# The second product of an MLP on four PSUM banks, one for each token tile, in place of three, and the first product on four in place of five

## The chip, the cores and the metric

The kernel runs on one core of a Trainium2 chip. The core has five engines that run side by side, each through its own list of instructions in order: TensorE (PE) for matrix products, VectorE (DVE) and GpSimd (POOL) for sums of tiles, ScalarE (ACT) for copies and nonlinear functions, and SyncE (SP), which here only issues transfers. An instruction waits for those of other engines through semaphores. Products of PE land in PSUM, which the kernel divides into eight banks of 128 x 512 fp32 values; the other tiles lie in SBUF, the on-chip memory.

The metric is the device time of one execution in microseconds (us); lower is better. Times are given as the median of several runs. One further execution is taken with a hardware profiler, and all rows below come from that one.

## What is computed

The model is a decoder layer: attention and a state space model side by side, then an MLP. The change lies in the MLP. Cut to that part, the reference is

```python
h = rmsnorm(x, pre_mlp_g[i]) * (1.0 + sc2) + sh2
f = jnp.square(jax.nn.relu(h @ w_mlp_in[i])) @ w_mlp_out[i]
x = x + g2 * rmsnorm(f, post_mlp_g[i])
```

with x of 1024 tokens x 1024 features, `w_mlp_in` 1024 x 4096 and `w_mlp_out` 4096 x 1024, all fp32.

## The kernel before

**Precision.** Each fp32 operand is split into a rounded part hi and the rest lo. `parts` (line 1081) does this: ACT copies the source to hi (line 1082), DVE subtracts to get lo (line 91, the helper `tt` that issues every sum). `mm3` (line 83) makes a product out of three matmuls, hi x hi, hi x lo and lo x hi (lines 86, 87, 88), which follow each other on PE. One call of `mm3` is called a product of three matmuls below.

**Pairs.** The 4096 hidden features are cut into 32 chunks of 128, and two chunks make a pair. Within a pair both matrix products of the MLP are done as a Strassen-Winograd scheme of 2 x 2 blocks: seven block products in place of eight, at the price of sums of blocks before and after. `pair_in(p)` (line 1171) makes the hidden features of pair p out of the first weight; its PSUM tiles are called `fi`, its weight blocks `w` (a ring of six), its raw weight tiles `w1r`. It gives the results to `f`: ACT copies, DVE adds, ACT takes relu and square. `BANK` (line 1168) says which of four accumulators a, b, c and f each block product goes to. a is in use from the first block product (P1) to the last but one (P4), whose result ACT reads at line 1215.

`pair_out(p)` (line 1330) multiplies the hidden features of pair p with the second weight. Its block products are numbered i = 0 to 6, and each has four token tiles t = 0 to 3: 28 steps (i,t) a pair, in the order of the list `STEPS`. Step (i,t) takes its operands from `ops[(7 p + i) % 3]` (two of these three buffers show as `ops` in the profile, the third as `h2s`), puts its product into the PSUM tile `q[t]`, shown as `fo`, and calls `collect`, which adds it to the running sum n of that token tile (`facc`):

```python
if first:
    q[t] = psR("BBD", "fo")
mm3(q[t], o[:, 0, 0, sl], o[:, 0, 1, sl], o[:, 1, 0], o[:, 1, 1], first, True, i != 4)
collect(q[t], i, t, n)
```

A tile is new only for i = 0, 2, 4 and 5. Products 1, 3 and 6 are accumulated on top of what products 0, 2 and 5 left in the same bank, so that bank serves two sums, and PE may add the second product only when the first sum has been read. `psR("BBD")` takes the banks in turn: two of pool B, one of pool D. So there are three banks for four token tiles, and the steps are arranged by `chain`: two token tiles of product 0, the same two of product 1, then the other two of each.

**Collecting.** `collect` has three ways. The first time a sum is touched, ACT copies it. Steps in the set `VIA`, seven of 28, go by ACT, which copies the bank to the one buffer `tmpc` (line 1325), and POOL, which adds `tmpc` to the sum. All others are one sum on DVE that reads the bank (facc<-facc,fo).

**Order of the work.** PE's order is written by hand (`manual_schedule`): the loop over pairs issues one step of `pair_out(p)` and then one piece of `pair_in(p + 1)`, one product of three matmuls each, in turn; at the start of a pair four pieces of `pair_in` come first. After the last token tile of product i, `convert` issues the splitting of the operands that are used three products later, the sums of blocks that these need (f<-f,f on DVE, w2r on POOL), and the next loads of the second weight on SP. The orders of the other engines are set by the scheduler of the framework at build time, each engine's list apart, from the order in which the program issues and from its own estimate of when things are ready.

Fourteen pairs go through `pair_out`. The last two pairs are added plainly in `mlp_last`, which takes its banks by the same counter as `psR("BBD")`.

Of the kernel before, what the change touches and what calls it, by code (L numbers as in the profile page):

```python
# [33 lines left out]
def tile_hymba(ctx: ExitStack, tc: tile.TileContext, x, c, w_ada, b_ada, pre_mix_g, w_in,  # L34
# [4 lines left out]
    V, A, PL, T, SY = nc.vector, nc.scalar, nc.gpsimd, nc.tensor, nc.sync  # L39
# [13 lines left out]
    def nm(s):  # L53
        cnt[0] += 1
        return f"{s}_{cnt[0]}"
# [4 lines left out]
    def slot(tag, shape, dt, name):  # L60
        return sp.tile(shape, dt, tag=tag, name=nm(name))
# [3 lines left out]
    def ps(tag, name="ps"):  # L65
        return pp.tile([P, 512], F32, tag=tag, name=nm(name), bufs=NBANK[tag])
# [3 lines left out]
    def psR(tags, name="pr"):  # L70
        rot[0] += 1
        return ps(tags[rot[0] % len(tags)], name)
# [10 lines left out]
    def mm3(ps, lh, ll, rh, rl, first, last, more=False):  # L83


        T.matmul(ps, lh, rh, start=first, stop=False, skip_group_check=more)  # L86
        T.matmul(ps, lh, rl, start=False, stop=False, skip_group_check=more)  # L87
        T.matmul(ps, ll, rh, start=False, stop=last, skip_group_check=more)  # L88

    def tt(e, o, a, b, op):  # L90
        e.tensor_tensor(o, a, b, op=op)  # L91
# [145 lines left out]
    fr, fi = par[:, 2], par[:, 3]  # L237
# [305 lines left out]
    while m < 16:  # L543
# [4 lines left out]
        t = R[:, 0:G * m].rearrange("p (g m) -> p g m", g=G)  # L548
# [19 lines left out]
    def gCd(t):  # L568
        return t.rearrange("p (g C d) -> p g C d", g=4, C=8)

    for qg in range(8):
# [13 lines left out]
        t = gCd(m2[:, qg % 2])  # L585
# [104 lines left out]
    for qg in range(8):  # L690
# [5 lines left out]
        t = (m2, m3)[qg % 2]  # L696
# [415 lines left out]
    def block(m):  # L1112
        return w1t[(m % RB) // 2][:, m % 2]

    def where(p, kind):
        return NB * (p - 1) + KIND.index(kind)
# [28 lines left out]
    def used(*ms):  # L1145
        ring["done"].update(ms)
        while ring["free"] in ring["done"]:
            ring["free"] += 1
        make_ahead()
# [5 lines left out]
    def f_blocks(p):  # L1155

        u_, v_ = ft[2 * (p % 2)], ft[2 * (p % 2) + 1]
        return u_[:, 0], u_[:, 1], v_[:, 0], v_[:, 1]

    def relu2(o):  # L1160
        A.activation(o, o, AF.Relu)  # L1161
        A.activation(o, o, AF.Square)
# [8 lines left out]
    def pair_in(p):  # L1171
        f11, f12, f21, f22 = f_blocks(p)
        q = {}
        for st, into in BANK.items():
            new = into not in q
            if new:
                q[into] = ps("C" if into == "f" else "A", "fi")
            if st[0] == "P":
                k, kind = PROD[st]
                m = where(p, kind)  # L1180
                b = block(m)
                for i in range(2):
                    mm3(q[into], b[:, 0, i], b[:, 1, i], hb[k][:, 0, i], hb[k][:, 1, i], new and i == 0,
                        i == 1, True)
                    if i == 0:
                        yield
                ms = (m,)
            else:
                m, h = where(p, st[0:2]), int(st[2])
                for i in range(4):  # L1190
                    b = block(m + i // 2)
                    mm3(q[into], b[:, 0, i % 2], b[:, 1, i % 2], hp[h][:, 0, i], hp[h][:, 1, i], new and i == 0,
                        i == 3, True)
                    if i < 3:
                        yield
                ms = (m, m + 1) if h else ()

            r = q[into]
            if st == "P1":
                A.activation(f12, r, AF.Copy)  # L1200
            elif st == "P2":
                tt(V, f11, r, f12, ADD)
                relu2(f11)
            elif st == "P6":
                A.activation(f21, r, AF.Copy)
            elif st == "P5":
                A.activation(f12, r, AF.Copy)
                tt(PL, f21, f21, f12, ADD)
            elif st == "P7":
                A.activation(f22, r, AF.Copy)  # L1210
            elif st == "P3":
                tt(V, f21, r, f21, ADD)
                relu2(f21)
            elif st == "P4":
                A.activation(f12, r, AF.Relu)
                A.activation(f12, f12, AF.Square)
            elif st == "Qb1":
                tt(V, f22, r, f22, ADD)
                relu2(f22)
            used(*ms)  # L1220
            yield
# [39 lines left out]
    NS = 7  # L1261

    def convert(n):

        p, i = n // NS, n % NS
        if p >= NP_:
            return
        F11, F12, F21, F22 = f_blocks(p)
        B11, B12, B21, B22 = [w2b[b] for b in ("B11", "B12", "B21", "B22")]
        o = ops[n % 3]  # L1270

        def pt(e, src):
            parts(o[:, e, 0], o[:, e, 1], src)

        if i == 0:
            pt(1, B11)
            pt(0, F11)
        elif i == 1:
            pt(1, B21)
            pt(0, F12)  # L1280
            tt(PL, B12, B22, B12, SUB)
            tt(V, F21, F11, F21, SUB)
        elif i == 2:
            pt(1, B12)
            pt(0, F21)
            tt(PL, B11, B12, B11, ADD)
            tt(PL, B21, B21, B11, SUB)
        elif i == 3:
            pt(1, B21)
            pt(0, F22)  # L1290
            w2_load(p + 1, "B11", B21)
            tt(PL, B12, B22, B11, SUB)
            tt(V, F21, F22, F21, SUB)
        elif i == 4:
            pt(1, B11)
            pt(0, F21)
            w2_load(p + 1, "B12", B11)
            tt(V, F11, F21, F11, ADD)
            tt(V, F12, F12, F21, SUB)
        elif i == 5:  # L1300
            pt(1, B12)
            pt(0, F11)
            w2_load(p + 1, "B22", B12)
        else:
            pt(1, B22)
            pt(0, F12)
            w2_load(p + 1, "B21", B22)
            w2b.update(B11=B21, B22=B12, B12=B11, B21=B22)

    def chain(i, na, nb):
        return [(i + e, t, (na, nb)[e]) for t0 in (0, 2) for e in range(2) for t in (t0, t0 + 1)]

    STEPS = chain(0, 1, 0) + chain(2, 4, 3) + [(4, t, 1) for t in range(4)] + chain(5, 4, 2)
    VIA = ((0, 1), (0, 3), (2, 1), (2, 3), (4, 1), (5, 1), (5, 3))
    seen = set()

    def collect(p_, i, t, n):
        a = acc[n][:, t]  # L1320
        if (n, t) not in seen:
            seen.add((n, t))
            A.activation(a, p_, AF.Copy)
        elif (i, t) in VIA:
            A.activation(tmpc, p_, AF.Copy)  # L1325
            tt(PL, a, a, tmpc, ADD)
        else:
            tt(V, a, a, p_, ADD)

    def pair_out(p):  # L1330
        q = {}
        for i, t, n in STEPS:
            o = ops[(NS * p + i) % 3]
            first = i in (0, 2, 4, 5)
            if first:
                q[t] = psR("BBD", "fo")
            sl = slice(t * P, (t + 1) * P)
            mm3(q[t], o[:, 0, 0, sl], o[:, 0, 1, sl], o[:, 1, 0], o[:, 1, 1], first, True, i != 4)
            collect(q[t], i, t, n)
            if t == 3:  # L1340
                convert(NS * p + i + 3)
            yield
# [72 lines left out]
    for b in ("B11", "B22", "B12", "B21"):  # L1415
        w2_load(0, b, w2b[b])
    g1 = pair_in(1)
    for _ in range(4):
        next(g1)
# [5 lines left out]
    for p in range(NP_):  # L1425
        g = pair_in(p + 1) if p else g1
        for _ in range(4 if p else 0):
            next(g)
        for _ in pair_out(p):
            next(g, None)  # L1430
        run(g)
    t = slot("B6", [P, 4, S], F32R, "f2w2")
    plain(NF - 4, (t[:, 0], t[:, 1]), (t[:, 2], t[:, 3]))
    t = hs[1][:, 0].rearrange("p a b t -> p a (b t)")
    t2_ = [slot(("S4", "G2S")[e], [P, D], F32R, "w2s") for e in range(2)]
    plain(NF - 3, (t[:, 0], t[:, 1]), t2_)
    run(pair_in(NP_ + 1))
    order.__exit__(None, None, None)
    for t in range(4):
        join(t)  # L1440
    for ci, tag in ((NF - 2, "B1"), (NF - 1, "B7")):
        t = slot(tag, [P, 4, S], F32R, "f2w2")
# [31 lines left out]
```

## Time and profile before

| quantity | value |
|---|---|
| median of 3 runs | 1195.97 us |
| the runs | 1197.16, 1195.97, 1181.49 us |
| profiled execution, its time | 1177.16 us |
| its span, first to last instruction | 1175.4 us |
| mean granted clock of TensorE | 0.983 |

The profile gives for each engine the time in which it was busy. Matmuls overlap: one takes 0.39 us from its start to its modelled end, and the next can start well before that end. The stage of the pairs shows in the page's strip of 40 slices (29.4 us each; a digit is the busy share in tenths), from slice 17 to slice 37:

```profile
PE   5889999699999998798999999999899899999896
DVE  3597895638754558878888888888878888888847
ACT  4553021858663655665455455454454454454441
POOL 5862000001022333553453453454444544543736
```

In an answer of the trace, `[0.59 <-DVE facc L91]` behind an instruction means that its engine was idle for 0.59 us before it and that the instruction of DVE at line 91 that writes `facc` came last of what it waited for. In a list of waits the form is: engine and line, what it waited for, total us, times, longest. In a list of groups it is: line, engine, operation, tiles and shapes, count | busy us, mean ns of one | idle us before them and their releasers.

### The profile page before, as it was taken

The numbers are of one execution on the slowest core, as the hardware profiler recorded it, in microseconds if no ns is written. First come the engines' busy times: TensorE is split into PE (matmuls) and PEld (weight loads), VectorE is DVE, ScalarE is ACT, GpSimd is POOL, SyncE is SP. The second block draws the span as 40 slices with busy tenths as digits, with TensorE's granted clock in tenths as the row PEclk, the third lists the DMA queues.
The fourth block names the chain that finished last, engine by engine and source line by source line (L and its number), as shares of the span: only waits on it lengthen the run. The fifth ranks groups of instructions, "written<-read, shape, count | busy, mean of one in ns | idle before, by whom it ended". The sixth has DMA issues, their size and how long they took to land.

```text
span 1175.4 us, 14665 instructions
## 1 busy us (share of the span) xinstructions
PE 1071.8 (91%) x5127; PEld 825.9 (70%) x5127; DVE 889.0 (76%) x1333; ACT 588.1 (50%) x1242; POOL 463.9 (39%) x420
## 2 busy tenths in 40 slices
PE   5889999699999998798999999999899899999896
PEld 3667777385667887686777777777677677677785
DVE  3597895638754558878888888888878888888847
ACT  4553021858663655665455455454454454454441
POOL 5862000001022333553453453454444544543736
PEclk9999999899999999899999999999999999999998
DMA  9956227300042323112012012012012012022126
GB/s 273 267 161 214 74 54 203 54 19 19 1 142 83 108 90 108 31 50 72 27 46 72 24 49 72 19 54 72 18 54 72 12 61 72 11 63 72 37 90 215
DMA packets 86592, 95.01 MB, mean 81 GB/s; under 512 B 21747, under 2 KB 65123, under 8 KB 86502
## 3 DMA queue, kind: packets, MB, share of 16 engines
q1 hardware_dynamic: 86182, 94.04, 26.5%
q8 instruction: 40, 0.66, 0.2%
q14 instruction: 34, 0.28, 0.1%
q10 hardware_dynamic: 240, 0.02, 0.0%
q0 software_dynamic: 96, 0.02, 0.0%
HBM read 83.96 MB, written 8.91 MB: 79 GB/s over the span
## 4 chain that ended last, share of the span: by engine, by line
DVE 23%; PE 13%; issue 6%; DMA 5%; ACT 5%; POOL 4%; DVEq 0%; POOLq 0%; SPq 0%; ACTq 0%
DVE facc L91 7%; DVE f L91 6%; DMA w1r<-in_w_mlp_in_dram 5%; DVE ops L91 4%; DVE w L91 3%; PE fo L86 3%; PE fo L87 2%; PE fo L88 2%; PE fi L86 2%; PE fi L87 2%; DVE h2s L91 2%; PE fi L88 2%; ACT ops L1082 1%; POOL w2r L91 1%; ACT w L1082 1%
## 5 line engine op out<-in xcount | busy, mean ns | idle before, releaser
L91 DVE TENSOR_TENSOR facc<-facc,fo 128x512 f32<-128x512 f32 x295 | 197.9, 676 | 33.6 <-PE fo L88 33.2
L91 POOL TENSOR_TENSOR facc<-facc,tmpc 128x512 f32<-128x512 f32 x94 | 137.0, 1457 | 160.7 <-ACT tmpc L1325 160.7
L1082 ACT ACTIVATE w<-w1r 128x256 fp32r<-128x256 f32 x169 | 69.3, 413 | 180.4 <-DMA w1r<-in_w_mlp_in_dram 78.1
L86 PE MATMUL fo<-ops 128*128 128x512 f32 x264 | 109.2, 414 | 29.3 <-DVE facc L91 28.5
L91 DVE TENSOR_TENSOR w<-w1r,w 128x256 fp32r<-128x256 f32 x169 | 95.3, 567 | 40.3 <-ACT w L1082 40.1
L87 PE MATMUL fo<-ops 128*128 128x512 f32 x264 | 103.4, 392 | 0.0
L88 PE MATMUL fo<-ops 128*128 128x512 f32 x264 | 103.4, 392 | 0.0
L88 PE MATMUL fi<-h,w 128*128 128x512 f32 x248 | 97.3, 392 | 6.4 <-DVE w L91 6.4
L86 PE MATMUL fi<-h,w 128*128 128x512 f32 x248 | 97.0, 391 | 0.0
L87 PE MATMUL fi<-h,w 128*128 128x512 f32 x248 | 96.9, 391 | 0.0
L86 PEld LDWEIGHTS fo<-ops 128*128 128x128 f32 x264 | 49.7, 188 | 62.5 <-DVE facc L91 36.0
L1325 ACT ACTIVATE tmpc<-fo 128x512 f32<-128x512 f32 x94 | 55.1, 587 | 43.5 <-PE fo L88 27.4
L91 DVE TENSOR_TENSOR ops<-f,ops 128x512 fp32r<-128x512 f32 x66 | 61.2, 927 | 20.7 <-ACT ops L1082 19.1
L91 POOL TENSOR_TENSOR w1r<-w1r 128x256 f32<-128x256 f32 x60 | 65.7, 1106 | 15.5 <-DMA w1r<-in_w_mlp_in_dram 8.2
L91 POOL TENSOR_TENSOR w2r<-w2r,w2r 128x512 f32<-128x512 f32 x35 | 49.6, 1418 | 48.8 <-DMA w2r<-in_w_mlp_out_dram 35.2
L86 PE MATMUL fo<-h2s 128*128 128x512 f32 x128 | 52.4, 410 | 13.5 <-DVE facc L91 13.2
L91 DVE TENSOR_TENSOR f<-f,f 128x512 f32<-128x512 f32 x42 | 64.1, 1552 | 0.0
L91 DVE TENSOR_TENSOR ops<-w2r,ops 128x512 fp32r<-128x512 f32 x66 | 61.1, 926 | 0.6 <-ACT ops L1082 0.6
L88 PEld LDWEIGHTS fi<-h,w 128*128 128x128 f32 x248 | 46.8, 189 | 16.9 <-DVE w L91 6.8
L88 PEld LDWEIGHTS fo<-ops 128*128 128x128 f32 x264 | 49.8, 188 | 10.9
L1161 ACT ACTIVATE f<-f 128x512 f32<-128x512 f32 x45 | 28.2, 628 | 57.7 <-DVE f L91 57.7
L87 PEld LDWEIGHTS fo<-ops 128*128 128x128 f32 x264 | 49.9, 189 | 7.6
(371 smaller groups left out, 2903.1 us busy)
## 6 DMA issues: line engine op xcount, KB each, us to landing
adm<-in_w_ada_dram SPq DMA_DIRECT2D x32, 512.0 KB
w2r<-in_w_mlp_out_dram SPq DMA_DIRECT2D x64, 256.0 KB
ad<-in_w_ada_dram SPq DMA_DIRECT2D x32, 256.0 KB
w1r<-in_w_mlp_in_dram SPq DMA_DIRECT2D x32, 256.0 KB
w1r<-in_w_mlp_in_dram SPq DMA_DIRECT2D x16, 512.0 KB
xn<-in_x_dram SPq DMA_DIRECT2D x8, 512.0 KB
xin<-in_x_dram SPq DMA_DIRECT2D x8, 512.0 KB
xs<-xin SPq DMA_DIRECT2D x8, 512.0 KB
```

The source lines that it names most:

```text
L86: T.matmul(ps, lh, rh, start=first, stop=False, skip_group_check=more)
L87: T.matmul(ps, lh, rl, start=False, stop=False, skip_group_check=more)
L88: T.matmul(ps, ll, rh, start=False, stop=last, skip_group_check=more)
L91: e.tensor_tensor(o, a, b, op=op)
L1082: A.activation(hi, src, AF.Copy)
L1161: A.activation(o, o, AF.Relu)
L1325: A.activation(tmpc, p_, AF.Copy)
```

## The change

The second product gets four banks, one for each token tile: two of pool B for t = 0 and 1, C for 2 and D for 3. Its products then go one after the other, each over all four token tiles, and no pairs of token tiles are needed. Bank C had held the accumulator f of the first product; this goes to pool A, so that the first product has the four banks of A for its four accumulators, where it had these and C. `VIA` becomes the diagonal (0,0), (1,1), (2,2), (3,3), (4,0), (5,1), (6,2).

```diff
             if new:
-                q[into] = ps("C" if into == "f" else "A", "fi")
+                q[into] = ps("A", "fi")
...
-    def chain(i, na, nb):
-        return [(i + e, t, (na, nb)[e]) for t0 in (0, 2) for e in range(2) for t in (t0, t0 + 1)]
-
-    STEPS = chain(0, 1, 0) + chain(2, 4, 3) + [(4, t, 1) for t in range(4)] + chain(5, 4, 2)
-    VIA = ((0, 1), (0, 3), (2, 1), (2, 3), (4, 1), (5, 1), (5, 3))
+    STEPS = [(i, t, n) for i, n in enumerate((1, 0, 4, 3, 1, 4, 2)) for t in range(4)]
+    VIA = [(i, i % 4) for i in range(NS)]
...
             if first:
-                q[t] = psR("BBD", "fo")
+                q[t] = ps("BBCD"[t], "fo")
```

The number of matmuls, of conversions and of loads stays. Over the whole kernel one sum goes from ACT and POOL to DVE, since a first touch in the first pair meets the diagonal at another place. What moves is the order.

On PE, the start of the 28 steps of pair 6 before, from the last matmul of step (0,0): numbers behind a name tell its uses apart, `fo` with one number is one bank.

```order
L88 MATMUL fo_584_5686<-ops_451_3580 128x512
L86 MATMUL fi_583_5679<-h2_358_2827,w1_442_3571 128x512
L87 MATMUL fi_583_5679<-h2_358_2827,w1_442_3571 128x512
L88 MATMUL fi_583_5679<-h2_358_2827,w1_442_3571 128x512
L86 MATMUL fo_585_5694<-ops_451_3580 128x512
L87 MATMUL fo_585_5694<-ops_451_3580 128x512
L88 MATMUL fo_585_5694<-ops_451_3580 128x512
L86 MATMUL fi_583_5679<-h2_358_2827,w1_442_3571 128x512
L87 MATMUL fi_583_5679<-h2_358_2827,w1_442_3571 128x512
L88 MATMUL fi_583_5679<-h2_358_2827,w1_442_3571 128x512
L86 MATMUL fo_584_5686<-ops_451_3580 128x512
```

The last row is step (1,0), on the bank of step (0,0). The same place on PE after the change:

```order
L88 MATMUL fo_584_5685<-ops_451_3580 128x512
L86 MATMUL fi_583_5678<-h2_358_2827,w1_442_3571 128x512
L87 MATMUL fi_583_5678<-h2_358_2827,w1_442_3571 128x512
L88 MATMUL fi_583_5678<-h2_358_2827,w1_442_3571 128x512
L86 MATMUL fo_585_5694<-ops_451_3580 128x512
L87 MATMUL fo_585_5694<-ops_451_3580 128x512
L88 MATMUL fo_585_5694<-ops_451_3580 128x512
L86 MATMUL fi_583_5678<-h2_358_2827,w1_442_3571 128x512
L87 MATMUL fi_583_5678<-h2_358_2827,w1_442_3571 128x512
L88 MATMUL fi_583_5678<-h2_358_2827,w1_442_3571 128x512
L86 MATMUL fo_586_5702<-ops_451_3580 128x512
```

The last row is now step (0,2), on a third bank; fo_584 comes again with step (1,0), four steps after (0,0).

On DVE, the change from pair 5 to pair 6 before, from the collection of step (6,3) on:

```order
L91 TENSOR_TENSOR facc_437_3566<-facc_437_3566,fo_581_5628 128x512
L91 TENSOR_TENSOR h2s_361_2830<-f_447_3576,h2s_361_2830 128x512
L91 TENSOR_TENSOR h2s_361_2830<-w2r_459_3687,h2s_361_2830 128x512
L91 TENSOR_TENSOR f_447_3576<-f_447_3576 128x512
L91 TENSOR_TENSOR facc_436_3565<-facc_436_3565,fo_584_5686 128x512
L91 TENSOR_TENSOR w1_443_3572<-w1r_444_3573,w1_443_3572 128x256
L91 TENSOR_TENSOR f_446_3575<-f_447_3576,f_446_3575 128x512
L91 TENSOR_TENSOR f_446_3575<-f_446_3575,f_447_3576 128x512
L91 TENSOR_TENSOR w1_441_3570<-w1r_444_3573,w1_441_3570 128x256
L91 TENSOR_TENSOR facc_436_3565<-facc_436_3565,fo_584_5686 128x512
L91 TENSOR_TENSOR facc_436_3565<-facc_436_3565,fo_585_5694 128x512
```

The collections are those of (0,0), in the midst of other sums, and of (1,0) and (1,1). The same place on DVE after the change:

```order
L91 TENSOR_TENSOR facc_437_3566<-facc_437_3566,fo_581_5613 128x512
L91 TENSOR_TENSOR h2s_361_2830<-f_447_3576,h2s_361_2830 128x512
L91 TENSOR_TENSOR h2s_361_2830<-w2r_459_3687,h2s_361_2830 128x512
L91 TENSOR_TENSOR f_447_3576<-f_447_3576 128x512
L91 TENSOR_TENSOR w1_443_3572<-w1r_444_3573,w1_443_3572 128x256
L91 TENSOR_TENSOR f_446_3575<-f_447_3576,f_446_3575 128x512
L91 TENSOR_TENSOR f_446_3575<-f_446_3575,f_447_3576 128x512
L91 TENSOR_TENSOR w1_441_3570<-w1r_444_3573,w1_441_3570 128x256
L91 TENSOR_TENSOR facc_436_3565<-facc_436_3565,fo_585_5694 128x512
L91 TENSOR_TENSOR facc_436_3565<-facc_436_3565,fo_586_5702 128x512
L91 TENSOR_TENSOR facc_436_3565<-facc_436_3565,fo_587_5710 128x512
```

(0,0) has gone to ACT and POOL, and the collections of (0,1), (0,2) and (0,3) stand in a row behind all other sums of this place.

On POOL, the middle of pair 6 before: facc<-facc,tmpc are the collections (2,1), (2,3) and (4,1), w2r is a subtraction on the second weight, w1r one on the first:

```order
L91 TENSOR_TENSOR facc_438_3567<-facc_438_3567,tmpc_450_3579 128x512
L91 TENSOR_TENSOR f_449_3578<-f_449_3578,f_448_3577 128x512
L91 TENSOR_TENSOR facc_438_3567<-facc_438_3567,tmpc_450_3579 128x512
L91 TENSOR_TENSOR w2r_459_3687<-w2r_459_3687 128x512
L91 TENSOR_TENSOR w1r_444_3573<-w1r_444_3573 128x2x128
L91 TENSOR_TENSOR facc_436_3565<-facc_436_3565,tmpc_450_3579 128x512
```

The same place on POOL after the change, where the collections are (2,2), (3,3) and (4,0):

```order
L91 TENSOR_TENSOR facc_438_3567<-facc_438_3567,tmpc_450_3579 128x512
L91 TENSOR_TENSOR f_449_3578<-f_449_3578,f_448_3577 128x512
L91 TENSOR_TENSOR w2r_459_3687<-w2r_459_3687 128x512
L91 TENSOR_TENSOR facc_437_3566<-facc_437_3566,tmpc_450_3579 128x512
L91 TENSOR_TENSOR w1r_444_3573<-w1r_444_3573 128x2x128
L91 TENSOR_TENSOR facc_436_3565<-facc_436_3565,tmpc_450_3579 128x512
```

The subtraction now stands ahead of the second collection, and the third collection belongs to the step right behind that of the second.

## The prediction

> **What bounds the kernel now.** I read the page first, then the busy time by stage, the timeline of TensorE (PE) and of VectorE (DVE), and last who waits for whom. On the page PE is the busiest engine, and DVE is next:
>
> ```profile
> PE 1071.8 (91%) x5127; PEld 825.9 (70%) x5127; DVE 889.0 (76%) x1333; ACT 588.1 (50%) x1242; POOL 463.9 (39%) x420
> L86 PE MATMUL fo<-ops x264: 389/389/628, 474.4 to 1098.7; 128*128 128x512 f32 x132
> ```
>
> The second row (the instructions on the tile fo) gives the stage that the change is in: the second product runs from 474.4 to 1098.7 us, 14 pairs of chunks, more than half of the span. The share of the whole span says little about it, so I cut five pairs out, from the first wait of one pair to the same wait of a later one (columns: stretch, its length, then busy time of PE, PEld, DVE, ACT and POOL, granted clock, DMA share, GB/s):
>
> ```profile
> 615.58:659.75 44.17, 41.26 (x174) 32.09 (x175) 37.84 (x54) 22.13 (x44) 20.97 (x17) 1.00 0.15 48
> ...
> 793.24:837.76 44.52, 41.27 (x174) 32.09 (x175) 37.66 (x54) 22.07 (x44) 20.82 (x17) 1.00 0.16 48
> sum 222.18, PE 206.32 PEld 160.44 DVE 189.50 ACT 110.36 POOL 104.85; mean PE 41.26 PEld 32.09 DVE 37.90 ACT 22.07 POOL 20.97
> ```
>
> A pair takes 222.18 / 5 = 44.4 us, has 174 matmuls and 189.50 / 5 = 37.9 us of DVE work, and the clock is full. What PE could do is read where nothing holds it, and what holds it from the rows with an idle time in brackets. All of pair 6 (pairs counted from 0):
>
> ```profile
> 748.66 0.47 PE L86 MATMUL fo<-ops 128*128 128x512 f32 x1 [0.59 <-DVE facc L91]
> 753.24 0.50 PE L86 MATMUL fo<-ops 128*128 128x512 f32 x1 [0.23 <-DVE facc L91]
> 755.37 0.50 PE L86 MATMUL fo<-ops 128*128 128x512 f32 x1 [0.47 <-DVE facc L91]
> 761.55 0.47 PE L86 MATMUL fo<-ops 128*128 128x512 f32 x1 [0.41 <-DVE facc L91]
> 767.54 0.50 PE L86 MATMUL fo<-ops 128*128 128x512 f32 x1 [0.26 <-DVE facc L91]
> 771.09 0.39 PE L86 MATMUL fi<-h,w 128*128 128x512 f32 x1
> ...
> 778.34 0.39 PE L88 MATMUL fi<-h2t,w 128*128 128x512 f32 x1
> 780.05 0.50 PE L86 MATMUL fo<-ops 128*128 128x512 f32 x1 [1.32 <-DVE facc L91]
> ```
>
> Between 771.09 and 778.34 lie 32 matmul starts, so a matmul is issued every 7.25 / 32 = 0.227 us, and 174 of them need 39.4 us. The other 5.0 us of the pair are waits. The six in brackets make 3.28 us; since an idle time is counted from a modelled end 0.39 us after the start, where the next matmul would have begun after 0.23, each is 0.16 longer: 4.2 us. The remaining 0.8 is spread over gaps too small to carry a label. All six are steps of the second product that wait for DVE to have read their PSUM bank. They are the steps (1,0), (0,3), (1,2), (3,0), (3,2) and (6,0), where (i,t) is product i, token tile t: five follow the last use of their bank by two steps, and (0,3) by three.
>
> DVE comes late for a reason that its own rows show, at the start of the pair:
>
> ```profile
> 744.44 1.19 DVE L91 TENSOR_TENSOR h2s<-f,h2s 128x512 fp32r<-128x512 f32 x1
> 745.55 1.22 DVE L91 TENSOR_TENSOR h2s<-w2r,h2s 128x512 fp32r<-128x512 f32 x1
> 746.70 1.22 DVE L91 TENSOR_TENSOR f<-f 128x512 f32<-128x512 f32 x1
> 747.84 0.68 DVE L91 TENSOR_TENSOR facc<-facc,fo 128x512 f32<-128x512 f32 x1
> 748.44 0.41 DVE L91 TENSOR_TENSOR w<-w1r,w 128x256 fp32r<-128x256 f32 x1
> 748.77 3.48 DVE L91 TENSOR_TENSOR f<-f,f 128x512 f32<-128x512 f32 x2
> 752.18 0.41 DVE L91 TENSOR_TENSOR w<-w1r,w 128x256 fp32r<-128x256 f32 x1
> 752.51 1.27 DVE L91 TENSOR_TENSOR facc<-facc,fo 128x512 f32<-128x512 f32 x2
> ```
>
> The collection at 747.84 ends at 748.52, and PE's step (1,0) starts at 748.66. DVE is not short of time over a pair, it has its work in bursts, and two steps of room are less than a burst.
>
> **The change part by part.** *Four banks, products one after the other.* From the end of a product to the next one on its bank lie three others of three matmuls now (9 x 0.227 = 2.0 us), and seven after (21 x 0.227 = 4.8 us). A collection may come 2.7 us later than it may now. The longest of the six waits is 1.32 + 0.16 = 1.5 us, so each of them goes if DVE is as late as it is now. At the burst: counted from the end of step (6,3) of the pair before, (1,1) starts after 14 products of 0.68 us, at 9.5 us. DVE has by then the collection of (6,3) with its start, 0.8 us, the burst from 744.44 to 752.51 without its collection, 8.07 - 0.60 = 7.5, and the collection of (0,1), 0.6: 8.9 us. It just fits, with 0.6 us to spare, if DVE carries no arrears into it.
>
> So PE's floor is 39.4 us, and what is late next is DVE as a whole. These rows are for the five pairs (engine, line, waited for: total, times, longest):
>
> ```profile
> DVE facc L91 <- PE fo L88: 11.3, 15, 1.1
> DVE w L91 <- ACT w L1082: 10.6, 12, 1.9
> DVE ops L91 <- ACT ops L1082: 7.3, 7, 1.2
> DVE h2s L91 <- ACT h2s L1082: 3.3, 3, 1.2
> ```
>
> Of DVE's 6.5 idle us a pair, 11.3 / 5 = 2.3 are waits for a PE that was itself held up; these go with the stalls. The waits for ACT are (10.6 + 7.3 + 3.3) / 5 = 4.2. If all of them stay, a pair cannot be shorter than 37.9 + 4.2 = 42.1; if none, PE's 39.4 bounds it. The largest is one wait:
>
> ```profile
> 761.33 1.47 DVE L91 TENSOR_TENSOR w<-w1r,w 128x256 fp32r<-128x256 f32 x1
> 766.46 0.43 DVE L91 TENSOR_TENSOR w<-w1r,w 128x256 fp32r<-128x256 f32 x1 [1.86 <-ACT w L1082]
> ```
>
> The first row frees a buffer, a load of the first weight fills it, ACT copies it, and the second row takes the rest. Two collections stand between the two rows in DVE's order before; after, it is three collections and the two h2s rows, some 2.4 us more work. I take this 1.9 us as covered and the rest as staying: 42.1 - 1.9 = 40.2.
>
> *DVE's rows that share POOL's time.* POOL's 21.0 us a pair are 47% of 44.4 us, and about 51% of the shorter pair. Three forms in the five pairs:
>
> ```profile
> L91 DVE TENSOR_TENSOR f<-f,f 128x512 f32<-128x512 f32 x15 | 23.3, 1580 | 0.0
> L91 DVE TENSOR_TENSOR ops<-f,ops 128x512 fp32r<-128x512 f32 x24 | 22.0, 917 | 7.3 <-ACT ops L1082 7.3
> L91 DVE TENSOR_TENSOR f<-fi,f 128x512 f32<-128x512 f32 x15 | 10.2, 680 | 0.0
> ```
>
> The same 128x512 sum takes 680 ns with an operand in PSUM and 917 to 1580 with both in SBUF. The excess of f<-f,f and of the 48 rows of ops is (15 x 0.90 + 48 x 0.24) / 5 = 5.0 us a pair; if it grows as POOL's share does, by a tenth at most, it costs 0.4 us. From below it costs nothing, and from above 0.5; I take 0.4.
> The Trainium skill (SBUF — State Buffer, section Who interferes with whom) says that a DVE instruction with two SBUF inputs contends with a GpSimd instruction that reads SBUF, and one with at most one SBUF input does not. The rows above agree, 680 against 917 and 1580 ns. It speaks against the change so far as a shorter pair packs the same POOL work closer: by the rule the 0.4 us belong in the sum, and by unchanged DVE rows the result would be 6 us lower.
>
> *The sums by way of ACT and POOL.* There are still seven a pair, one less in all (in the first pair), 0.6 us of DVE: nothing. But they stood four steps apart, and now (3,3) and (4,0) follow each other through the one buffer tmpc, with a subtraction on the second weight ahead of the first of them on POOL. Rows of pair 6, the group of the copies, and ACT's wait for that buffer in the five pairs:
>
> ```profile
> 766.21 0.39 PE L88 MATMUL fo<-h2s 128*128 128x512 f32 x1
> 768.24 1.74 POOL L91 TENSOR_TENSOR facc<-facc,tmpc 128x512 f32<-128x512 f32 x1
> 774.38 1.29 POOL L91 TENSOR_TENSOR w2r<-w2r 128x512 f32<-128x512 f32 x1 [4.40 <-DMA w2r<-in_w_mlp_out_dram]
> L1325 ACT ACTIVATE tmpc<-fo 128x512 f32<-128x512 f32 x94 | 55.1, 587 | 43.5 <-PE fo L88 27.4
> ACT tmpc L1325 <- POOL facc L91: 3.1, 3, 1.2
> ```
>
> That subtraction starts 774.38 - 766.44 = 7.9 us after the end of step (2,3). From that end, (5,0), which takes over the bank of (4,0), is 17 products or 11.6 us away. POOL: 7.9 + 1.3 for the subtraction, then 1.3 to 1.7 for (3,3): 10.5 to 10.9; ACT's copy of (4,0), 0.6: 11.1 to 11.5. So (5,0) has 0.1 to 0.5 us to spare, but ACT stands for up to 3 us, and its rows behind it (squares of f, halves of ops) come later, and DVE with them. Between 0 and 3 us I take 0.2, near the low end, because PE is clear of it and DVE has its collections to do meanwhile.
>
> *The rest.* The bank of a pair's (first product's) P4 is now taken by the next pair's P1, where there was a spare one. In the trace ACT has read P4 long before:
>
> ```profile
> 778.77 0.59 ACT L1215 ACTIVATE f<-fi 128x512 f32<-128x512 f32 x1
> 787.05 0.39 PE L86 MATMUL fi<-h2s,w 128*128 128x512 f32 x1
> ```
>
> 7.7 us lie between, and a faster PE takes 1 to 2 of them: nothing; without that cover P1 would wait for ACT. The conversions of operands are issued after every fourth step in place of two close together and a long pause; the loads on SP's queue keep their order; and the counter that picks the banks of the last stage misses 224 turns, a multiple of its 8. All nothing.
>
> *Sum.* 40.2 + 0.4 + 0.2 = 40.8 us a pair, 3.6 less than 44.4; 14 pairs give 50 us. The profiled execution took 1177.16 us (span 1175.4), so 1127. The three timed runs before lie 4.3, 18.8 and 20.0 above it, 14 on the mean, for which no row gives a reason; with these 14 the forecast is 1141.
>
> **The rivals.** *PE alone bounds* (0.17): DVE's waits for ACT were only the slack of an engine ahead of PE, and the pair falls to 39.4. Then 5.0 x 14 = 70, 1107 + 14 = 1121. For it: four steps of room even out bursts; against it: DVE would have to be busy 38.3 of 39.4 us.
> *DVE keeps all its waits for ACT* (0.20): 42.1 + 0.4 = 42.5, a gain of 1.9 x 14 = 27, so 1150 + 14 = 1164. For it: ACT and DVE are in order, and a load's time does not shrink with PE. With another 0.5 us of waits it is within 2%.
> *The waits only move* (0.07): PE finds its bank free and waits for ops or w instead, 44.4 again: 1191. Against it: in five pairs no row of PE names any of these; each half of an operand is now asked for eight steps ahead, where it was four at the shortest.
> *Slower, by tmpc* (0.06): ACT, held at (4,0), makes DVE idle. It is decided at 44.4 - 42.5 = 1.9 us of new idle time a pair on top of the rival before last. If the wait of POOL's subtraction for its load, 4.4 us, reaches DVE whole, the pair takes 46.9 us, 35 us more in all: 1177 + 35 + 14 = 1226. Against it: DVE's collections do not go through ACT.
>
> **How the numbers follow.** My forecast has 0.50, the rivals 0.17, 0.20, 0.07 and 0.06. A measurement of this kernel tells about 2% from no change, which is 1172 against the median of 1196. Faster by more: 0.50 + 0.17 + 0.12 of the 0.20 = 0.79; within 2%: 0.08 + 0.07 = 0.15; slower 0.06. The range goes from 1111 (PE alone, with the 4 us of the nearest run) to 1172 (DVE's waits kept, with 20 in place of 14, and a little more), which leaves out the last two rivals and part of the third.
>
> **What would show it.** Right: a pair takes 40 to 42 us between the same rows; PE's waits for DVE facc fall from 3 us a pair to under 1; DVE is busy over 90% of a pair; its waits for PE are nearly gone. The cover of the w wait shows as a wait below 1 us on that row. Wrong: if tmpc counts, ACT's waits for POOL facc rise from under 1 us a pair to 3, with DVE ops waiting behind; if P4's bank counts, the first matmul of a pair on fi waits for ACT L1215. If PE's waits for facc stay, DVE's arrears at the burst are larger than I took them, and the forecast is wrong by them.

## The result, and the profile after

| quantity | before | after |
|---|---|---|
| median, of 4 runs each | 1188.73 us | 1133.36 us |
| the runs | 1181.4, 1181.49, 1195.97, 1197.16 us | 1123.89, 1124.39, 1142.33, 1143.18 us |
| profiled execution, its time | 1177.16 us | 1142.33 us |
| its span | 1175.4 us | 1140.5 us |
| mean granted clock of TensorE | 0.983 | 0.963 |

The ratio is 0.9454, with a 95% interval of 0.9309 to 0.9599: the changed kernel is faster by about 5%. The runs of either kernel lie in two groups, about 15 us apart before and 18 after, which go with TensorE's clock in a stretch ahead of the stage of the change (the last section shows it), so from here on I compare pairs, and the stage of the 14 pairs.

From the page of the kernel after, its busy times and the chain of work that ended last, and the row of the instructions on the tile fo:

```profile
PE 1070.9 (94%) x5127; PEld 842.5 (74%) x5127; DVE 882.6 (77%) x1334; ACT 588.7 (52%) x1241; POOL 449.9 (39%) x419
PE 60%; DVE 18%; DMA 7%; POOL 6%; issue 5%; ACT 3%; SPq 1%; DVEq 0%; POOLq 0%; ACTq 0%
L86 PE MATMUL fo<-ops x264: 388/390/629, 493.5 to 1062.2; 128*128 128x512 f32 x132
```

The busy times are nearly those of before, with 14 pairs in 568.7 us (493.5 to 1062.2) in place of 624.3: 55.6 us less. The chain runs over PE for 60% of the span. The span shrank by only 34.9 us, because the stage begins 19.1 us later than in the profile of before, and 1.6 us came up behind it. The pairs by themselves, cut from step (1,1) of one pair to (1,1) of the next (columns as in the same view of before):

```profile
588.64:628.90 40.26, 39.73 (x174) 32.60 (x174) 37.38 (x54) 22.15 (x44) 19.97 (x16) 1.00 0.18 53
628.90:669.78 40.88, 39.73 (x174) 32.60 (x175) 38.37 (x54) 21.92 (x44) 20.52 (x16) 1.00 0.17 52
...
sum 242.78, PE 238.46 PEld 195.58 DVE 226.69 ACT 132.44 POOL 121.58; mean PE 39.74 PEld 32.60 DVE 37.78 ACT 22.07 POOL 20.26
```

A pair takes 242.78 / 6 = 40.46 us, where it was 44.44: 3.98 less, and 14 times that, 55.7, is the 55.6 us of the stage. The granted clock is 1.00 in all these pairs, before and after. DVE has as much work in it as before, 37.78 against 37.90. What is waited for in these six pairs (engine, line, waited for: total us, times, longest):

```profile
DVE facc L91 <- PE fo L88: 6.6, 13, 0.7
PE fo L86 <- DVE facc L91: 4.8, 7, 1.1
DVE w L91 <- ACT w L1082: 3.9, 8, 0.9
DVE ops L91 <- ACT ops L1082: 2.4, 6, 0.7
POOL w2r L91 <- DMA w2r<-in_w_mlp_out_dram: 2.1, 4, 0.9
DVE h2s L91 <- ACT h2s L1082: 1.9, 4, 0.7
```

PE waits for a collection seven times (the first and the last are the two ends of the cut), 0.5 to 1.1 us each and once a pair, where pair 6 of before had 3.28 by the same labels. All of them are now at one step, (1,1), the first one behind DVE's burst at the start of a pair. On PE in pair 6, the first matmuls of steps (6,3) of pair 5 and of (1,1), with the last matmul ahead of the latter:

```profile
739.46 0.39 PE L86 MATMUL fo<-h2s 128*128 128x512 f32 x1
...
749.43 0.39 PE L88 MATMUL fi<-h,w 128*128 128x512 f32 x1
750.34 0.50 PE L86 MATMUL fo<-ops 128*128 128x512 f32 x1 [0.53 <-DVE facc L91]
```

Unhindered, (1,1) would have begun 0.227 us after 749.43, at 749.66; it begins 0.68 later. DVE at the same place, from the collection of (6,3) at 740.63 to those of (0,1), (0,2) and (0,3) at 749.62:

```profile
740.29 0.41 DVE L91 TENSOR_TENSOR w<-w1r,w 128x256 fp32r<-128x256 f32 x1
740.63 0.68 DVE L91 TENSOR_TENSOR facc<-facc,fo 128x512 f32<-128x512 f32 x1
741.59 1.73 DVE L91 TENSOR_TENSOR h2s<-f,h2s 128x512 fp32r<-128x512 f32 x1 [0.29 <-ACT h2s L1082]
743.25 1.23 DVE L91 TENSOR_TENSOR h2s<-w2r,h2s 128x512 fp32r<-128x512 f32 x1
744.40 1.23 DVE L91 TENSOR_TENSOR f<-f 128x512 f32<-128x512 f32 x1
745.55 1.51 DVE L91 TENSOR_TENSOR w<-w1r,w 128x256 fp32r<-128x256 f32 x1
746.98 2.38 DVE L91 TENSOR_TENSOR f<-f,f 128x512 f32<-128x512 f32 x2
749.28 0.41 DVE L91 TENSOR_TENSOR w<-w1r,w 128x256 fp32r<-128x256 f32 x1
749.62 1.87 DVE L91 TENSOR_TENSOR facc<-facc,fo 128x512 f32<-128x512 f32 x3
```

The first of the three collections, on the bank that (1,1) wants, ends at 749.62 + 0.68 = 750.30, and PE goes on at 750.34. The burst between the collections lasts from 741.59 to 749.62, 8.03 us. The same w row takes 0.41 us at 749.28 and 1.51 at 745.55. What POOL does meanwhile:

```profile
740.78 0.74 POOL L91 TENSOR_TENSOR w1r<-w1r 128x256 f32<-128x256 f32 x1 [1.90 <-DVE w L91]
741.48 1.29 POOL L91 TENSOR_TENSOR facc<-facc,tmpc 128x512 f32<-128x512 f32 x1
742.73 2.34 POOL L91 TENSOR_TENSOR w1r<-w1r 128x256 f32<-128x256 f32 x2
745.03 1.74 POOL L91 TENSOR_TENSOR w2r<-w2r,w2r 128x512 f32<-128x512 f32 x1
746.74 1.47 POOL L91 TENSOR_TENSOR facc<-facc,tmpc 128x512 f32<-128x512 f32 x1
```

POOL is busy without a gap from 740.78 to 748.21, through nearly the whole burst. The DVE row at 749.28, behind that, is the short one.

### The profile page after: what moved, and what is told of

It reads as the page before. It is cut to its first block, busy times and chain, and to the rows that moved or that the text cites. A ratio compares the mean times of both kernels' runs of the same rounds, so it can differ in the third digit from the quotient of the medians.

```text
span 1140.5 us, 14650 instructions
## 1 busy us (share of the span) xinstructions
PE 1070.9 (94%) x5127; PEld 842.5 (74%) x5127; DVE 882.6 (77%) x1334; ACT 588.7 (52%) x1241; POOL 449.9 (39%) x419
## 4 chain that ended last, share of the span: by engine, by line
PE 60%; DVE 18%; DMA 7%; POOL 6%; issue 5%; ACT 3%; SPq 1%; DVEq 0%; POOLq 0%; ACTq 0%
PE fo L86 7%; PE fo L87 7%; PE fo L88 7%; PE fi L88 6%; PE fi L87 6%; PE fi L86 6%; DVE f L91 4%; DVE facc L91 2%; PE po L1001 2%; PE po L1002 2%; PE po L1004 2%; DVE w L91 2%; DMA adm<-in_w_ada_dram 2%; PE vp L580 2%; POOL w1r L91 2%
## 5 line engine op out<-in xcount | busy, mean ns | idle before, releaser
L91 DVE TENSOR_TENSOR facc<-facc,fo 128x512 f32<-128x512 f32 (+1 forms) x296 | 196.5, 677 | 25.5 <-PE fo L88 25.2
L91 POOL TENSOR_TENSOR facc<-facc,tmpc 128x512 f32<-128x512 f32 x93 | 128.0, 1377 | 133.6 <-ACT tmpc L1322 133.3
L91 DVE TENSOR_TENSOR w<-w1r,w 128x256 fp32r<-128x256 f32 x169 | 117.1, 696 | 11.4 <-ACT w L1082 10.6
L86 PE MATMUL fo<-ops 128*128 128x512 f32 x264 | 104.2, 395 | 4.3 <-DVE facc L91 4.3
L88 PE MATMUL fo<-ops 128*128 128x512 f32 x264 | 103.4, 392 | 0.0
L87 PE MATMUL fo<-ops 128*128 128x512 f32 x264 | 103.3, 391 | 0.0
L91 POOL TENSOR_TENSOR w1r<-w1r 128x256 f32<-128x256 f32 x60 | 58.7, 987 | 40.7 <-DVE w L91 31.9
L91 POOL TENSOR_TENSOR w2r<-w2r,w2r 128x512 f32<-128x512 f32 x35 | 52.0, 1487 | 43.9 <-issue 30.9
L1082 ACT ACTIVATE ops<-f 128x512 fp32r<-128x512 f32 x66 | 41.5, 629 | 48.4 <-PE fo L87 45.5
L91 DVE TENSOR_TENSOR ops<-f,ops 128x512 fp32r<-128x512 f32 x66 | 56.0, 848 | 12.6 <-ACT ops L1082 9.2
L91 DVE TENSOR_TENSOR ops<-w2r,ops 128x512 fp32r<-128x512 f32 x66 | 55.3, 838 | 0.5 <-ACT ops L1082 0.3
L1001 PE MATMUL po<-woh,hd 128*128 128x512 f32 x128 | 51.6, 404 | 3.4 <-ACT mix L1006 2.4
```

The source lines that it names most:

```text
L1001: T.matmul(p_, hd[v][h][:, 0, i, o:o + P], woh[v][:, i, sl], start=i == 0, stop=False)
L1082: A.activation(hi, src, AF.Copy)
```

## The experiments

Each is told by the pair, cut at the same step each time. "Ordinary pair" is the first of the pairs cut. It is one of the shorter ones: in the kernel after, two of the six pairs are longer by 0.5 to 0.6 us, those at whose end the wait at (1,1) is 1.1 in place of 0.5 us. So for the kernels in the new order the stage is given beside it: the 14 pairs, from the first to the last start in the row of fo as shown above, 568.7 us in the kernel after. In e3, e4 and e5 one pair has a granted clock of 0.96 and is 1.6 us longer by that; this is in their stages.

**e1: only the first product's bank.** The kernel before, with f in pool A and nothing else changed.

```diff
-                q[into] = ps("C" if into == "f" else "A", "fi")
+                q[into] = ps("A", "fi")
```

> One part alone: the first product's accumulator f goes to pool A (four banks for its four accumulators), the second product stays on its three banks in the old order. My theory (PE waits because a bank of the second product is asked for again after two steps, before DVE has read it): no change, within 4 us of before, six waits on DVE facc a pair, 44.4 us a pair. Rival (the first product's part of the change brings a share of the gain, or the loss of its spare bank costs): a pair shorter or longer than 44.4 by over 0.3 us, or a wait of PE on fi for ACT L1215.

Measured: 1197.33 us median of 4 runs, beside 1197.57 of the kernel before (7 runs), and five pairs in all (the sum line of the view by pairs):

```profile
sum 222.21, PE 206.18 PEld 160.45 DVE 190.01 ACT 110.26 POOL 105.57; mean PE 41.24 PEld 32.09 DVE 38.00 ACT 22.05 POOL 21.11
```

222.21 / 5 = 44.44, the pair of before to a hundredth, with the same five or six labelled waits. Four banks in place of five cost the first product nothing, and give nothing.

**e2: four banks, old order.** A bank for each token tile of the second product, but the old `STEPS` and `VIA`.

```diff
-                q[into] = ps("C" if into == "f" else "A", "fi")
+                q[into] = ps("A", "fi")
...
-                q[t] = psR("BBD", "fo")
+                q[t] = ps("BBCD"[t], "fo")
```

> Four banks for the second product, one for each token tile, and f in pool A, but the old order of its steps (two token tiles of a product, the same two of the next) and the old set VIA. My theory (what counts is the room in steps between two uses of a bank, not the number of banks): five of the six waits stay, since (1,0), (1,2), (3,0), (3,2) and (6,0) still come two steps after the last use; only (0,3), 0.4 us, goes. Pair about 44.0 us, whole kernel 0 to 8 us faster. Rival (a fourth bank is what was missing): most of the gain, a pair under 41.5 us, 40 us or more faster.

Measured: 1179.1 to 1196.23 us in 4 runs, beside 1177.37 to 1199.68 of the kernel before; the ratio is 1.0049 (0.9909 to 1.0188). The sum of five pairs:

```profile
sum 222.12, PE 204.79 PEld 160.85 DVE 189.91 ACT 110.55 POOL 105.04; mean PE 40.96 PEld 32.17 DVE 37.98 ACT 22.11 POOL 21.01
```

222.12 / 5 = 44.42: no gain, where I had expected 0.4 us. PE in pair 6 of this kernel, two of its five waits:

```profile
749.69 0.47 PE L86 MATMUL fo<-ops 128*128 128x512 f32 x1 [0.59 <-DVE facc L91]
...
756.39 0.50 PE L86 MATMUL fo<-ops 128*128 128x512 f32 x1 [0.98 <-DVE facc L91]
```

The first is (1,0). The wait of (0,3), the one that shared a bank for lack of a fourth, is gone, and that of (1,2), the second row, is 0.98 where (1,2) had waited 0.47. So what holds PE is not the number of banks, but how many steps lie between two uses of the same bank. A bank more, with products still accumulated two steps later, only moved a wait here.

**e3: old choice of collections.** The kernel after with the old set `VIA`, which splits the work of the new order otherwise between DVE and ACT with POOL.

```diff
-    VIA = [(i, i % 4) for i in range(NS)]
+    VIA = ((0, 1), (0, 3), (2, 1), (2, 3), (4, 1), (5, 1), (5, 3))
```

> The changed kernel with the old set VIA, (0,1), (0,3), (2,1), (2,3), (4,1), (5,1), (5,3), in place of the diagonal. My theory: which seven sums go by ACT and POOL matters little; the pair stays within 0.7 us of the 40.4 of the changed kernel, 0 to 10 us either way, and the one wait that is left moves with the collection that it waits for. Rival (the diagonal spreads the load of DVE and POOL and carries a good part of the gain): a pair of 42 us or more, 20 us slower than the changed kernel.

Measured: 1151.56 us median of 4 runs beside 1197.57. The ordinary pair, and PE's wait in pair 7:

```profile
587.21:628.31 41.10, 39.73 (x174) 32.58 (x174) 36.83 (x54) 22.15 (x44) 20.35 (x17) 1.00 0.17 52
...
795.68 0.50 PE L86 MATMUL fo<-h2s 128*128 128x512 f32 x1 [1.33 <-DVE facc L91]
```

The pair is 41.10, 0.84 above that of the kernel after, and there is again one wait a pair, at (1,0) now: the collection of (0,0), which the diagonal gives to ACT and POOL, is back on DVE, behind the burst, and (1,0) comes two products earlier than (1,1). So most of the gain, 44.4 to 41.1, belongs to the order and the banks together, and the diagonal adds 0.8 us a pair. That is a little more than I had allowed it. The stage takes 579.8 us (493.1 to 1072.9), 11.1 more than that of the kernel after. Two of its pairs are long: 42.68 us at the lower clock, and before it 42.60 at the full clock, with a wait of 2.85 us at its end, for which nothing was run. The diagonal in the old order was not run either.

**e4: one sum of the burst moved to POOL.**

```diff
-            tt(V, F12, F12, F21, SUB)
+            tt(PL, F12, F12, F21, SUB)
```

> The changed kernel with one of the two long sums of f in DVE's burst at the start of a pair (F12 less F21) given to POOL. My theory (the one wait that is left in a pair, 0.68 us at step (1,1), is the end of that burst): DVE is done 1.2 us sooner, the wait goes, a pair takes 39.6 to 39.9 us, the kernel is 7 to 11 us faster than the changed one. Rival (POOL's list becomes the bound, its subtraction rows come late and ACT stands at the buffer of the sums): no gain, or up to 20 us slower, with waits of ACT for POOL facc above 1 us a pair.

Measured: 1150.44 us median of 4 runs beside 1197.57. The ordinary pair, and of the burst DVE's first row and those behind the first w row, with POOL's last:

```profile
588.35:629.12 40.77, 39.76 (x174) 32.59 (x174) 37.48 (x53) 22.15 (x44) 21.90 (x17) 1.00 0.18 52
```

```profile
744.87 1.73 DVE L91 TENSOR_TENSOR h2s<-f,h2s 128x512 fp32r<-128x512 f32 x1 [0.29 <-ACT h2s L1082]
...
750.26 1.77 DVE L91 TENSOR_TENSOR f<-f,f 128x512 f32<-128x512 f32 x1
751.95 1.51 DVE L91 TENSOR_TENSOR w<-w1r,w 128x256 fp32r<-128x256 f32 x1
753.39 1.87 DVE L91 TENSOR_TENSOR facc<-facc,fo 128x512 f32<-128x512 f32 x3
...
751.44 1.75 POOL L91 TENSOR_TENSOR facc<-facc,tmpc 128x512 f32<-128x512 f32 x1
```

My theory missed here: with a row less the burst should have been shorter and the wait at (1,1) gone. The burst is longer, 8.52 us (744.87 to 753.39) for 8.03, the wait at (1,1) is 1.02 for 0.53, and the pair is 0.51 longer; the stage takes 576.7, 8.0 longer. The rival had allowed for this time, but not by this way: no row of ACT waits for POOL's collections in this kernel's list of waits. The second w row, 0.41 in the kernel after, takes 1.51, and POOL is still at work beside it, from 751.44 to 753.19. This made me look at the burst as DVE's and POOL's work together, and led to the last experiment, e7.

**e5 and e6: one row more, in the burst and elsewhere.** The subtraction that makes the low half of an operand is done a second time, with the same operands, once for product 2 and once for product 4. The first copy falls into the burst, the second behind the collection of (2,0), in the middle of the pair.

```diff
         elif i == 2:
             pt(1, B12)
             pt(0, F21)
+            tt(V, o[:, 0, 1], F21, f32(o[:, 0, 0]), SUB)
```

> The changed kernel with one row of DVE done twice (the same subtraction of one half of an operand, the same values), in the burst at the start of a pair. By itself such a row takes 0.6 us. My theory (the burst fills all the room that four steps give, with a wait of 0.68 us at (1,1) left): the wait grows by what the row takes there, 0.6 us alone to 1.2 us beside POOL, and the pair from 40.4 to 41.0 to 41.6 us. Rival (DVE has 2.6 us to spare in a pair, so one row more costs nothing wherever it stands): pair within 0.2 us of 40.4.

```diff
         elif i == 4:
             pt(1, B11)
             pt(0, F21)
+            tt(V, o[:, 0, 1], F21, f32(o[:, 0, 0]), SUB)
```

> The changed kernel with the same kind of row done twice in the middle of a pair, behind the collection of (2,0), in place of its start. My theory (bursts bound, not DVE's work over a pair): no wait of PE appears there and the pair stays within 0.2 us of 40.4, though DVE has the same extra work as with the row at the start. Rival (DVE's total work bounds the pair): 0.6 to 1.2 us longer, as with the row at the start.

Measured, one run each: 1155.13 and 1141.89 us. The ordinary pair with the row in the burst:

```profile
593.51:634.38 40.87, 39.73 (x174) 32.59 (x174) 37.80 (x55) 22.15 (x44) 20.07 (x16) 1.00 0.16 52
```

its burst from end to end, and PE's wait behind it, at pair 6:

```profile
749.92 1.73 DVE L91 TENSOR_TENSOR h2s<-f,h2s 128x512 fp32r<-128x512 f32 x1 [0.29 <-ACT h2s L1082]
...
758.55 1.87 DVE L91 TENSOR_TENSOR facc<-facc,fo 128x512 f32<-128x512 f32 x3
...
759.28 0.50 PE L86 MATMUL fo<-ops 128*128 128x512 f32 x1 [1.13 <-DVE facc L91]
```

and the ordinary pair with the row in the middle:

```profile
588.60:628.86 40.26, 39.73 (x174) 32.58 (x174) 37.73 (x55) 22.16 (x44) 20.05 (x16) 1.00 0.17 53
```

DVE has 55 rows in both and is busy as long, 37.80 and 37.73. In the burst the row costs the pair 0.61 us, all of it at (1,1), whose wait goes from 0.53 to 1.13; in the middle it costs nothing, 40.26 as without it. The stages say the same, 577.7 and 567.9 beside 568.7. So DVE's total does not bound the pair, and what stands between the collection of (6,3) and that of (0,1) adds to it. In the middle, in pair 6 of the kernel after, DVE is idle for 0.51 us ahead of the collection of (2,3), waiting for PE; with the added row this wait is gone. Other places were not tried.

**e7: a sum of POOL's moved into DVE's burst.** A subtraction on the second weight, POOL's row of 1.74 us at 745.03 above, goes to DVE.

```diff
-            tt(PL, B12, B22, B11, SUB)
+            tt(V, B12, B22, B11, SUB)
```

> The changed kernel with the subtraction on the second weight that POOL does in the burst (1.74 us there) given to DVE. What failed with a sum of f on POOL gives two theories. Contention (in the burst a row of POOL and a DVE row with two operands in SBUF take turns, so POOL's rows stretch the burst by their own length): DVE has 0.6 us more work but is stretched 1.3 to 1.7 us less, the wait at (1,1) falls from 0.68 to under 0.3 us, a pair takes 39.7 to 40.1 us, the kernel is 4 to 9 us faster than the changed one. Rival (the burst is DVE's own work): the wait grows by 0.6 us, a pair takes 41.0 us, 8 us slower than the changed one.

Measured: 1127.76 us median (1117.68, 1119.28, 1136.25 and 1136.44), beside 1176.59 to 1197.9 of the kernel before. Six pairs, and of the burst DVE's first row, POOL's last, and DVE's rows behind the first w row:

```profile
sum 239.30, PE 238.48 PEld 195.51 DVE 222.80 ACT 132.59 POOL 112.37; mean PE 39.75 PEld 32.59 DVE 37.13 ACT 22.10 POOL 18.73
```

```profile
722.42 1.73 DVE L91 TENSOR_TENSOR h2s<-f,h2s 128x512 fp32r<-128x512 f32 x1 [0.30 <-ACT h2s L1082]
...
725.86 1.74 POOL L91 TENSOR_TENSOR facc<-facc,tmpc 128x512 f32<-128x512 f32 x1
...
727.80 0.68 DVE L91 TENSOR_TENSOR w2r<-w2r,w2r 128x512 f32<-128x512 f32 x1
728.40 1.28 DVE L91 TENSOR_TENSOR f<-f,f 128x512 f32<-128x512 f32 x2
729.61 0.41 DVE L91 TENSOR_TENSOR w<-w1r,w 128x256 fp32r<-128x256 f32 x1
729.94 1.87 DVE L91 TENSOR_TENSOR facc<-facc,fo 128x512 f32<-128x512 f32 x3
```

DVE does one sum more in each pair and is busy for 37.13 us in place of 37.78. The two f<-f,f take 1.28 us for 2.38, with POOL idle beside them (its last row ends at 727.60), and the burst, 722.42 to 729.94, is 7.52 us with the added row in it. A pair is 239.30 / 6 = 39.88 us, 0.58 below the kernel after, and (1,1) carries a label in one pair of six. The stage takes 562.2 us (476.7 to 1038.9), 6.5 less: the quickest kernel of this study. It ran beside the kernel before, not beside the kernel after.

Three of these kernels differ from the kernel after by one row in or beside the burst, and pair and burst move together. The burst is that at the start of pair 6, and the pair is the one that ends with it, at (1,1) of pair 6:

| kernel | burst | pair | 14 pairs |
|---|---|---|---|
| after | 8.03 | 40.26 | 568.7 |
| a sum to POOL (e4) | 8.52 (+0.49) | 40.80 (+0.54) | 576.7 (+8.0) |
| a row more in the burst (e5) | 8.63 (+0.60) | 40.87 (+0.61) | 577.7 (+9.0) |
| a sum from POOL (e7) | 7.52 (-0.51) | 39.85 (-0.41) | 562.2 (-6.5) |

The last one gains less than its burst, because (1,1) is then only 0.24 us late, and PE's own 39.4 us come next.

## Why the prediction was right, and where it was not

**Time.** 1141 was forecast and 1133.36 measured, inside the range of 1111 to 1172. The sum for the profiled execution, at a mean clock of 0.983, was 1127; the two runs after that come near this clock, 0.979 and 0.980, took 1124. The gain was forecast as 50 us and is 55.6. The median of 1133.36 lies between two runs of 1124 and two of 1142 to 1143, so how near it comes to 1141 hangs on how many runs had the lower clock; that part is luck.

**The room of four steps.** Right, and shown: e2 has the banks without the room and gains nothing, and in the kernel after, with the room, all six waits are gone. The one that is left, at (1,1), is at a step that did not wait before.

**The burst at (1,1).** This was walked at the right place and sized wrong: 0.6 us to spare became 0.68 of wait. From the end of (6,3), 0.68 after 739.46, the collection of (6,3) was to be through in 0.8 us; it ended after 1.17, because a w row stood ahead of it on DVE. Then DVE stood 0.28 for ACT. These are the arrears on whose absence the step of the prediction rested. And the burst was 8.03 for 7.5: h2s 1.73 for 1.19, the first w row 1.51 for 0.41, and f<-f,f 2.38 for 3.48. I had taken the burst's length over from the trace of before, as if its rows had durations of their own. The term of the sum that was missing for this is 0.68 us a pair at (1,1).

**DVE's waits for ACT as the bound.** The number came near, 40.2 + 0.6 = 40.8 against 40.46, but the mechanism was wrong, so this nearness is luck too. Waits for ACT are (3.9 + 2.4 + 1.9) / 6 = 1.4 us a pair, where I had left 2.3, and e6 shows that DVE has room for more work. DVE's waits for PE, which I had forecast as nearly gone, are still 6.6 / 6 = 1.1 us a pair, as on an engine that is not the limit. What bounds a pair is PE, 39.4 + 0.68 = 40.1 and a little that carries no label: the rival "PE alone bounds", with what is left of the burst. I argued against it that DVE would have to be busy 38.3 of 39.4 us, 97%. In e7 it is busy 37.13 of 39.88, 93%, with PE hardly held up; whether 97% would do, no run shows.

**The w wait.** Right: the rows of DVE waiting for ACT's w are 0.9 us at most, where 1.86 was one wait of before.

**DVE's rows beside POOL, 0.4 us.** Wrong as a term on DVE's total, which fell from 37.90 to 37.78. But the sharing decides the length of the burst, by e4 and e7, and the 0.68 us of wait stands in its place. The Trainium skill (SBUF — State Buffer, section Who interferes with whom) names the two-input DVE row and GpSimd's read as what contend. The trace agrees: facc<-facc,fo, with one operand in PSUM, keeps its 0.68 us at 740.63 beside a POOL row, and w<-w1r,w does not.

**tmpc, 0.2 us.** No cost shows. POOL's subtraction waits for its load 2.1 / 6 = 0.35 us a pair, where one such wait was 4.40 before, and the list has no wait of ACT for POOL's collections. Why the load is there in time now, nothing was run to show.

**P4's bank.** Right: e1 leaves the pair at 44.44, and the list of the kernel after has no wait of PE for ACT at fi.

**The 14 us between the profiled execution and the runs.** They have a likely reason now, the clock of the last section: the profile of before has the full clock there, and where it is half, the stage begins 16 to 25 us later. Which of the three runs had it, no trace shows; the 14 is a mean of 4.3, 18.8 and 20.0.

## What to carry to other kernels

Count the room between two uses of a PSUM bank in time, and set it against the longest burst in the queue of the engine that empties it: a bank more did nothing while the next use still came two steps later (e2). The length of a burst is not a property of its instructions: look at what POOL does beside two-operand sums on DVE before moving work from one to the other, because the move that takes a sum off DVE (e4) lengthened its burst, and the one that gives it a sum (e7) shortened it.

## What the runs showed of the hardware

**A low clock well inside the program, in some executions.** Busy time and granted clock of PE in two stretches of 20 us, long before the second product, in the kernel after:

```profile
120.00:140.00 20.00, 20.00 (x91) 11.75 (x90) 10.19 (x15) 0.00 (x0) 0.00 (x0) 0.50 0.34 103
140.00:160.00 20.00, 20.00 (x97) 14.21 (x98) 11.93 (x21) 0.00 (x0) 0.00 (x0) 0.65 0.01 3
```

and the first of them in the kernel before:

```profile
120.00:140.00 20.00, 20.00 (x149) 13.83 (x149) 16.99 (x25) 0.00 (x0) 0.00 (x0) 1.00 0.27 82
```

PE is busy without a break in both, with 91 matmuls at a clock of 0.50 and 149 at 1.00, and one matmul of this stretch (vp<-U,F, line 580) takes 0.42 us at the median in the first and 0.28 in the second. This is code that the change does not touch. The profiles of e1, e3, e4, e5 and e6 show the lower clock there too, and in these and the kernel after the second product begins at 492.9 to 498.9 us. Those of e2 and e7 show the full clock, and in these and the kernel before it begins at 474.4 to 476.7. So this stretch goes with a start 16 to 25 us later. The pair at 0.96 in e3, e4 and e5 is a smaller case in the stage itself: PE is busy 1.6 us longer in it with the same matmuls. Why the clock is low in one execution and full in the next stays open.

**DVE and POOL side by side.** In the burst a 128x256 sum takes 0.41 us with POOL idle and 1.51 beside it, and two 128x512 sums 1.28 and 2.38. By estimate, at 0.60 us for each of the five larger sums and 0.34 for each of the two smaller ones, the spacing of rows that follow each other undisturbed, DVE's burst of 8.03 us would need 3.7. That POOL's presence lengthens DVE's rows, e7 shows; that the two take turns row by row is only my reading of the lengths.
